# Nearest-neighbour upsampling: rows owned in two blocks, loads of 8, 252 and 252 rows, stores of at most 63 rows

## The chip, the cores and the metric

The kernel runs on one core of a Trainium2 chip. The metric is the device time of one execution in microseconds. Before the change three runs gave 197.04, 197.16 and 197.44 us, so the median is 197.16 us.

## The reference

Each element of `x` (16 × 64 × 64 × 64, float32) is written to a 2 × 2 square of the result, which is 16 × 64 × 128 × 128:

```python
for i in range(new_h):
    for j in range(new_w):
        src_i = i // scale_factor
        src_j = j // scale_factor
        result[:, :, i, j] = x[:, :, src_i, src_j].copy()
```

The input has 16.78 MB and the result 67.11 MB. Nothing is calculated: the work is moving bytes.

## The kernel before

The three outer dimensions of `x` are taken together into 65,536 rows of 64 elements (256 bytes). Each of the 128 partitions owns 512 rows that follow one another in memory. One row of `x` gives two rows of the result with 128 elements each, 1,024 bytes in all, so what a partition writes is contiguous as well: 512 × 1,024 bytes.

*Loads.* SyncE (SP) issues three loads: 8, 248 and 256 rows a partition (the cuts 0, 8, 256, 512). `begin_before_barrier` moves these three issues ahead of the barrier at the program's start.

*Copies.* VectorE (DVE) expands rows with a `tensor_copy` whose source repeats each element twice and each row twice (steps of 0), and whose destination is one dense stretch. A copy of k rows writes k × 256 elements a partition. The sizes stand in `rows`: 62, 32, 48, 64, 50, 64, 64, 64, 64. The first entry is copied in two halves, of 31 and 31 rows (`parts`). So there are ten copies. In this text copy 0 means the pair of 31 rows, and copy 1 to copy 8 are the others in order; store 0 to store 8 are the stores of what they wrote.

*Stores.* SP issues a store when the last copy into it is done, nine in all. Loads and stores share one queue and run in the order of their issue.

*Memory.* One SBUF tile `mem` holds a working area of 79 expanded rows and behind it all 512 source rows. Copies with an even number write at its start; copies with an odd number write a stretch that ends where the source rows that are not yet used begin. Two neighbours never overlap, but copy n overlaps what store n-2 reads, so copy n waits until store n-2 has landed. DVE runs the copies in order, so copy n also waits for copy n-1. Store n waits for copy n. In this way a copy has about the time of one store, that of number n-1, to be done before the queue runs empty.

`close_early` shortens the program's end and isn't touched.

Of the kernel before, what the change touches and what calls it, by code (L numbers as in the profile page):

```python
# [1 line left out]

# [4 lines left out]

EARLY = 3  # L10


def begin_before_barrier(nc):

    blocks = nc.main_func.blocks
    main, body = blocks[0], blocks[1]
    sp = mybir.EngineType.SP
    loads = [i for i in body.instructions if i.engine == sp][:EARLY]  # L20
    for load in loads:
        assert isinstance(load, mybir.InstDMACopy), type(load)
        assert not (load.sync_info and load.sync_info.on_wait)
    names = [i.name for i in loads]
    body.instructions = [i for i in body.instructions if i.name not in names]
    kept = list(main.instructions)
    at = next(
        n
        for n, i in enumerate(kept)
        if i.engine == sp and isinstance(i, mybir.InstDrain)  # L30
    )
    kept[at:at] = loads
    main.instructions = kept


def close_early(nc):

    blocks = nc.main_func.blocks  # L40
    sp, pool = mybir.EngineType.SP, mybir.EngineType.Pool
    stores = [
        i
        for i in blocks[1].instructions
        if i.engine == sp and isinstance(i, mybir.InstDMACopy)
    ]
    last = stores[-1].sync_info.on_update[0].id

    end = list(blocks[-1].instructions)
    wait = end[0]  # L50
    assert wait.engine == sp and isinstance(wait, mybir.InstDrain)
    waits = list(wait.sync_info.on_wait)
    assert len({w.id for w in waits}) == len(waits) > 2
    assert all(w.wait_mode == "sem-ge-imm" for w in waits)

    mine = [i for i in end if i.engine == pool]
    kinds = [type(i).__name__ for i in mine]
    assert kinds == [
        "InstDrain",
        "InstEventSemaphore",  # L60
        "InstEventSemaphore",
        "InstDrain",
        "InstISA",
        "InstDrain",
        "InstEventSemaphore",
        "InstEventSemaphore",
    ], kinds
    d0, gather0, release0, d1, clear, d2, gather1, release1 = mine


    lo, hi = clear.ant_dict["range_first"], clear.ant_dict["range_last"]
    assert lo <= last <= hi and all(lo <= w.id <= hi for w in waits)
    clears = []
    for a, b in ((lo, last), (last + 1, hi + 1)):
        if a < b:
            clears.append(nc.gpsimd.sem_clear(range(a, b)).ins)

    landed = mybir.InstDrain(
        name=wait.name,
        engine=pool,  # L80
        debug=wait.debug,
        sync_info=mybir.SyncInfo(
            on_wait=[w for w in waits if w.id != last], on_update=[]
        ),
    )
    (w,) = [w for w in waits if w.id == last]
    final = mybir.InstEventSemaphore(
        name=clear.name,
        engine=sp,
        debug=wait.debug,  # L90
        sync_info=mybir.SyncInfo(
            on_wait=[w],
            on_update=[
                mybir.SyncUpdate(
                    sync_type=w.sync_type,
                    id=w.id,
                    ant_name=w.ant_name,
                    update_mode="sem-sub-imm",
                    update_value=w.wait_value,
                )  # L100
            ],
        ),
    )
    others = [i for i in end if i.engine != pool and i is not wait]
    blocks[-1].instructions = others + [
        d0, gather0, release0, gather1, release1, d1, landed, *clears, d2, final
    ]


@with_exitstack  # L110
def kernel(
    ctx: ExitStack,
    tc: tile.TileContext,
    x: bass.AP,
    scale_factor: int,
    out: bass.AP,
):
    nc = tc.nc
    nc.at_finalize(begin_before_barrier)
    nc.at_finalize(close_early)  # L120
    P = nc.NUM_PARTITIONS
    s = int(scale_factor)
    B, C, H, W = x.shape
    R = B * C * H // P
    fdt = x.dtype

    xp = x.rearrange("b c h w -> (b c h) w").rearrange("(p r) w -> p r w", p=P)
    op = out.rearrange("b c (h hd) w -> (b c h) (hd w)", hd=s).rearrange(  # L130
        "(p r) w -> p r w", p=P
    )

    rows = [62, 32, 48, 64, 50, 64, 64, 64, 64]
    GROW = s * s
    FREE = 79
    WF = FREE * GROW * W  # L140
    assert sum(rows) == R
    mem_pool = ctx.enter_context(tc.tile_pool(name="mem", bufs=1))
    mem = mem_pool.tile([P, WF + R * W], fdt, name="mem")
    xt = mem[:, WF:].rearrange("p (r w) -> p r w", r=R)

    HEAD = 8
    cuts = [0, HEAD, R // 2, R]
    for lo, hi in zip(cuts, cuts[1:]):  # L150
        nc.sync.dma_start(out=xt[:, lo:hi], in_=xp[:, lo:hi])  # L151

    def expanded(r0, r1):
        return (
            xt[:, r0:r1].unsqueeze(2).unsqueeze(4).to_broadcast([P, r1 - r0, s, W, s])
        )

    r0 = 0
    before = (0, 0)
    for n, k in enumerate(rows):  # L160
        size = k * GROW * W
        at = 0 if n % 2 == 0 else WF + r0 * W - size
        assert at >= before[1] or at + size <= before[0]
        before = (at, at + size)
        u = mem[:, at : at + size].rearrange(
            "p (k a w b) -> p k a w b", k=k, a=s, w=W
        )
        parts = [0, 31, k] if n == 0 else [0, k]
        for a, b in zip(parts, parts[1:]):
            nc.vector.tensor_copy(out=u[:, a:b], in_=expanded(r0 + a, r0 + b))  # L170
        nc.sync.dma_start(out=op[:, r0 : r0 + k, :], in_=u)
        r0 += k


# [1 line left out]
_INS = ['x', 'scale_factor']  # L176
_OUTS = [((16, 64, 128, 128), 'float32')]

_NUMBERS = {'scale_factor': 2}


# [26 lines left out]
```

## Time and profile before

| what | value |
|---|---|
| time, median of three runs | 197.16 us |
| span of the profiled execution, first to last instruction | 195.8 us |
| what lies around the span (197.16 − 195.8) | 1.36 us |
| DVE busy | 78.0 us (40%), 10 copies |
| DMA, share of the 16 engines' time | 99.2% |
| DMA, bytes and mean rate | 83.89 MB, 428 GB/s |

For the profiled execution the page states its span alone; its own time, with what lies around the span, is not given, so the median of the three runs stands for it and the difference is taken as 1.36 us.

The page's numbers come from one execution. Its line on the DMA shows 40 equal slices of the span, and each digit is the busy share in tenths. The timeline lists instructions in order of time and merges neighbours of one kind ("x3"); in square brackets stands how long the engine had been idle before, and what released it. An SP row covers the issuing instructions, not the transfers.

### The profile page before, as it was taken

To read this page: it belongs to the slowest core of one execution; us is meant where nothing else is said; L and a number is where in the kernel's file an instruction comes from. 1 tells how busy PE (TensorE), PEld (TensorE's weight loads), DVE (VectorE), ACT (ScalarE), POOL (GpSimd) and SP (SyncE) were. 2 spreads that over 40 slices of the span, in tenths; PEclk is the share of its full clock that TensorE was granted. 3 is DMA by queue.
4 is the path that set the end of the run, shared out by engine and by line. 5 is a ranking of instruction groups with operands and counts; after the bars stand their busy time and mean duration, and the time that the engine had idled before them with its cause. 6 is when DMAs were issued, how large, how long until landed. Compare 5 with 4: busy or idle time off the path is not lost.

```text
span 195.8 us, 76 instructions
## 1 busy us (share of the span) xinstructions
DVE 78.0 (40%) x10; POOL 0.2 (0%) x4
## 2 busy tenths in 40 slices
DVE  0000599980007579085008907900890088000000
POOL 0000000000000000000000000000000000000000
DMA  9999999999999999899987989999999999999994
GB/s 456 415 428 415 428 428 428 428 415 415 415 415 428 428 482 482 375 469 495 469 384 345 502 348 455 442 469 482 469 442 428 428 428 442 428 428 428 428 428 214
DMA packets 1728, 83.89 MB, mean 428 GB/s; under 512 B 192, under 2 KB 192, under 8 KB 320
## 3 DMA queue, kind: packets, MB, share of 16 engines
q1 hardware_dynamic: 1728, 83.89, 99.2%
HBM read 16.78 MB, written 67.11 MB: 428 GB/s over the span
## 4 chain that ended last, share of the span: by engine, by line
DMA 60%; DVE 24%; SPq 0%; issue 0%; DVEq 0%
DMA out_dram<-mem 49%; DVE mem L170 24%; DMA mem<-in_x_dram 11%; SPq L151 0%; DVEq L170 0%
## 5 line engine op out<-in xcount | busy, mean ns | idle before, releaser
L170 DVE COPY mem<-mem 128x16384 f32<-128x16384 f32 (+4 forms) x10 | 78.0, 7812 | 87.8 <-DMA out_dram<-mem 65.8
L189 POOL MEMSET const-uint8-127<- 128x1 uint8 x1 | 0.1, 102 | 0.0
L189 POOL MEMSET const-bfloat16-1.0<- 128x1 bf16 x1 | 0.1, 101 | 0.0
L189 POOL MEMSET const-float32-0.0<- 128x1 f32 x1 | 0.1, 98 | 0.2 <-issue 0.2
L189 POOL MEMSET const-float32-1.0<- 128x1 f32 x1 | 0.1, 98 | 0.0
## 6 DMA issues: line engine op xcount, KB each, us to landing
mem<-in_x_dram SPq DMA_DIRECT2D x1, 7936.0 KB, 21.5
out_dram<-mem SPq DMA_DIRECT2D x1, 7936.0 KB, 21.2
out_dram<-mem SPq DMA_DIRECT2D x1, 6400.0 KB, 27.6
out_dram<-mem SPq DMA_DIRECT2D x1, 6144.0 KB, 17.5
out_dram<-mem SPq DMA_DIRECT2D x1, 4096.0 KB, 26.4
mem<-in_x_dram SPq DMA_DIRECT2D x1, 256.0 KB, 2.7
out_dram<-mem SPq DMA_DIRECT2D x5, 29.8
mem<-in_x_dram SPq DMA_DIRECT2D x1, 40.4
```

The costliest lines, as they stand in the source:

```text
L170: nc.vector.tensor_copy(out=u[:, a:b], in_=expanded(r0 + a, r0 + b))
L189: nc = _bacc.Bacc("TRN2", target_bir_lowering=False, num_devices=1)
```

## The change

The rows of `x` are cut into two parts. Of the first 128 × 260 rows each partition owns 260 that follow one another; of the other 128 × 252 rows each owns 252. So a partition's two stretches lie far apart in memory, and the distance between neighbouring partitions' stretches is 260 or 252 rows in place of 512. The loads become 8, 252 and 252 rows, and the sizes in `rows` become 62, 32, 52, 63, 51, 63, 63, 63, 63. The first five add up to 260, so no store crosses from one block into the other, and the number of loads (three), copies (ten) and stores (nine) is what it was. `within` cuts a stretch of rows at the blocks' border and returns the view of each piece.

```diff
-    xp = x.rearrange("b c h w -> (b c h) w").rearrange("(p r) w -> p r w", p=P)
-    op = out.rearrange("b c (h hd) w -> (b c h) (hd w)", hd=s).rearrange(
-        "(p r) w -> p r w", p=P
-    )
...
+    xr = x.rearrange("b c h w -> (b c h) w")
+    outr = out.rearrange("b c (h hd) w -> (b c h) (hd w)", hd=s)
+    BLOCKS = [260, 252]
+    assert sum(BLOCKS) == R
+    xb, ob, r0 = [], [], 0
+    for k in BLOCKS:
+        xb.append(xr[P * r0 : P * (r0 + k)].rearrange("(p r) w -> p r w", p=P))
+        ob.append(outr[P * r0 : P * (r0 + k)].rearrange("(p r) w -> p r w", p=P))
+        r0 += k
+
+    def within(views, lo, hi):
+        found, r0 = [], 0
+        for k, v in zip(BLOCKS, views):
+            a, b = max(lo, r0), min(hi, r0 + k)
+            if a < b:
+                found.append((a, b, v[:, a - r0 : b - r0]))
+            r0 += k
+        return found
+
+    rows = [62, 32, 52, 63, 51, 63, 63, 63, 63]
-    rows = [62, 32, 48, 64, 50, 64, 64, 64, 64]
...
-    HEAD = 8
-    cuts = [0, HEAD, R // 2, R]
-    for lo, hi in zip(cuts, cuts[1:]):
-        nc.sync.dma_start(out=xt[:, lo:hi], in_=xp[:, lo:hi])
+    LOADS = [0, 8, 260, R]
+    for lo, hi in zip(LOADS, LOADS[1:]):
+        for a, b, part in within(xb, lo, hi):
+            nc.sync.dma_start(out=xt[:, a:b], in_=part)
...
-        nc.sync.dma_start(out=op[:, r0 : r0 + k, :], in_=u)
+        for a, b, part in reversed(within(ob, r0, r0 + k)):
+            nc.sync.dma_start(out=part, in_=u[:, a - r0 : b - r0])
```

## The prediction

> **What bounds the kernel now.** I read the page's header first, then the slices and the DMA queue.
>
> ```profile
> span 195.8 us, 76 instructions
> DVE 78.0 (40%) x10; POOL 0.2 (0%) x4
> DVE  0000599980007579085008907900890088000000
> DMA  9999999999999999899987989999999999999994
> q1 hardware_dynamic: 1728, 83.89, 99.2%
> ```
>
> The 16 DMA engines are busy for 99.2% of the span, in every slice. DVE is busy for 40%. So the time is that of moving 83.89 MB, and a copy costs nothing as long as its store is issued before the queue runs empty. The question is therefore how much room each copy has. The timeline shows it.
>
> ```profile
> 0.00 1.32 SPq L151 DMA_DIRECT2D mem<-in_x_dram  x3
> 21.99 21.21 DVE L170 COPY mem<-mem 128x7936 f32<-128x7936 f32 x3 [21.99 <-DMA mem<-in_x_dram]
> 38.77 127.47 SPq L171 DMA_DIRECT2D out_dram<-mem  x9
> 59.98 6.56 DVE L170 COPY mem<-mem 128x12288 f32<-128x12288 f32 x1 [16.78 <-DMA out_dram<-mem]
> 69.70 8.70 DVE L170 COPY mem<-mem 128x16384 f32<-128x16384 f32 x1 [3.17 <-DMA out_dram<-mem]
> 84.12 6.83 DVE L170 COPY mem<-mem 128x12800 f32<-128x12800 f32 x1 [5.72 <-DMA out_dram<-mem]
> 103.54 8.69 DVE L170 COPY mem<-mem 128x16384 f32<-128x16384 f32 x1 [12.60 <-DMA out_dram<-mem]
> 118.55 8.69 DVE L170 COPY mem<-mem 128x16384 f32<-128x16384 f32 x1 [6.31 <-DMA out_dram<-mem]
> 137.94 8.70 DVE L170 COPY mem<-mem 128x16384 f32<-128x16384 f32 x1 [10.69 <-DMA out_dram<-mem]
> 157.19 8.69 DVE L170 COPY mem<-mem 128x16384 f32<-128x16384 f32 x1 [10.55 <-DMA out_dram<-mem]
> ```
>
> Each of the last seven rows begins when a store lands: copy 2 at the landing of store 0 (59.98), copy 3 at that of store 1 (69.70), and so on. From 59.98 to the end at 195.8 the queue moves the eight stores 1 to 8, 32+48+64+50+4×64 = 450 rows, so a stored row costs (195.8 − 59.98) / 450 = 0.3018 us. A row is 128 × 1,024 bytes, so that is 434 GB/s. A store of 64 rows takes 19.3 us and the copy beside it 8.7. The room is large.
>
> **The price of a copy.** This decides the case. The groups by shape:
>
> ```profile
> L170 DVE COPY mem<-mem 128x16384 f32<-128x16384 f32 x5 | 43.5, 8694 | 43.3 <-DMA out_dram<-mem 43.3
> L170 DVE COPY mem<-mem 128x7936 f32<-128x7936 f32 x2 | 16.7, 8414 | 22.0 <-DMA mem<-in_x_dram 22.0
> L170 DVE COPY mem<-mem 128x12800 f32<-128x12800 f32 x1 | 6.8, 6827 | 5.7 <-DMA out_dram<-mem 5.7
> L170 DVE COPY mem<-mem 128x12288 f32<-128x12288 f32 x1 | 6.6, 6561 | 16.8 <-DMA out_dram<-mem 16.8
> L170 DVE COPY mem<-mem 128x8192 f32<-128x8192 f32 x1 | 4.4, 4427 | 0.0
> ```
>
> Compare the second row with the last: 31 rows (7,936 elements) take 8,414 ns, 32 rows (8,192 elements) take 4,427 ns. Less work, almost twice the time. The rows with 64, 50, 48 and 32 rows lie on one line: slope (8694 − 4427) / (16384 − 8192) = 0.5209 ns an element, and 4427 − 8192 × 0.5209 = 160 ns fixed. With the same 160 ns the 31-row copies cost (8414 − 160) / 7936 = 1.040 ns an element, twice as much. The four fast sizes are even and the slow one is odd; all have the same line, types and source pattern, and the DMA is busy beside all of them. So I read it as: an odd number of rows halves DVE's rate. The change makes five copies of 63 rows and one of 51, both odd. By the odd rate 63 rows (16,128 elements) take 160 + 16128 × 1.040 = 16.94 us, where the even rate would give 8.56; 51 rows (13,056) take 13.74 instead of 6.96; 52 rows, even, take 7.09. The trace has only one odd size, so the lower bound of the price is the even rate, which gives the first rival.
>
> The Trainium skill says in "VectorE: DVE Perf Modes", section "What auto-detection actually checks", that a one-source copy in SBUF gets its two-elements-a-cycle mode if the outermost dimensions of source and destination are both even, or equal. Here the source's outermost count is the number of rows and the destination is one dense run, so by that rule 63 and 51 rows fall out of the mode as 31 do, and 62 rows in one copy would not. The rule reaches the sizes 63 and 51 that the trace doesn't show, and speaks against the change; by it the sum below stays as it is, and were the 31-row price a matter of size alone, the sum would be nothing.
>
> **What the change does not move.** Bytes, and the numbers of loads, copies and stores, stay the same. With the queue full, rows cost the same in any cut, so the new sizes by themselves cost nothing on the DMA. Load 2 has four rows more, at a quarter of a stored row's bytes each: 4 × 0.3018 / 4 = 0.30 us later, so copy 0 ends and store 0 is issued 0.30 us later, at 39.07. Load 3 covers that:
>
> ```profile
> L151 SPq DMA_DIRECT2D mem<-in_x_dram x3: 380/420/432, 0.0 to 0.9; - x3
> mem<-in_x_dram SPq DMA_DIRECT2D x1, 256.0 KB, 2.7
> mem<-in_x_dram SPq DMA_DIRECT2D x1, 40.4
> ```
>
> It is issued at 0.9 and lands 40.4 later, at 41.3, before and after alike, since the three loads together have the same bytes. The landings of stores 0 and 1, near 59.98 and 69.70, stay where they are. Were that cover gone, the price would be the 0.30 us. Copy 2 grows from 48 to 52 rows and ends at 59.98 + 7.09 = 67.07, while store 1 lands at about 69.63 (59.97 + 32 × 0.3018): covered too.
>
> **The price of an empty queue.** The trace of before never shows the queue run dry behind a store; the nearest case is the start. The first load is issued at 0.0 and lands at 2.7; its 256 KB are 0.60 us at 434 GB/s, which leaves 2.15 us on top (with 2.75 for the rounded 2.7). That is the upper bound, since it fetches from HBM with nothing in flight. The lower bound is the first packet alone, without a landing:
>
> ```profile
> DMA  0000000000000000000000000000000009929069
> ```
>
> These are 40 slices of the first 1.2 us: packets begin in slice 34, at 1.0 us. So a store into an empty queue pays L = 1.0 to 2.15 us, from its issue, beyond its rows. I take 1.6, the middle: it has a landing to wait for, which the lower bound leaves out, but reads SBUF and not HBM.
>
> **The sum, store by store.** A copy starts 0.08 us after the landing it waits for (the page's rows lie between 0.03 and 0.10: load 2's landing to 21.99 in the chain below, and 59.95 to 59.98), and its store is issued 0.03 after its end.
>
> ```profile
> 0.43 21.46 DMA mem<-in_x_dram
> 21.89 0.03 issue
> 21.99 16.76 DVE mem L170 x2
> 38.77 21.19 DMA out_dram<-mem
> 59.98 6.57 DVE mem L170
> 66.56 17.53 DMA out_dram<-mem
> ```
>
> - Copy 3 (63 rows) starts at 69.70 with store 1's landing and ends at 86.64; store 3 is issued at 86.67. Store 2 (52 rows) has landed at 69.63 + 52 × 0.3018 = 85.32. The queue is empty: store 3 counts from 86.67 + 1.6 = 88.27, which is 2.95 us late. It lands at 88.27 + 63 × 0.3018 = 107.29.
> - Copy 4 (51 rows) waits for copy 3 and ends at 100.39, while store 3 still runs: covered by 5.3 us. Store 4 lands at 107.29 + 15.39 = 122.68.
> - Copy 5 (63 rows) waits for store 3's landing, runs 107.37 to 124.30, issue 124.33. Store 4 has landed at 122.68. Empty again: 124.33 + 1.6 − 122.68 = 3.25 us late. Store 5 lands at 144.95.
> - Copy 6 waits for copy 5 (store 4 has landed) and ends at 141.25: covered by 2.1 us. Store 6 lands at 163.96.
> - Copies 7 and 8 wait for stores 5 and 6. Each turn takes 0.08 + 16.94 + 0.03 + 1.6 = 18.65 us against a store of 19.01: covered, by only 0.37 us.
>
> Two stalls, 2.95 + 3.25 = 6.2 us. They do not hide each other, for the queue has no spare time anywhere. The span becomes 195.8 + 6.2 = 202.0, and with the 1.36 us around it (median 197.16 less span 195.8) the time is 203.4 us. With L = 1.0 the sum is 1.35 + 1.65 + 2 × 1.0 = 5.0, time 202.2. With L = 2.15 it is 7.3, and copy 7 loses its cover too, by 0.18 us (copy 8 then has the late store 7 beside it): 7.5, time 204.7.
>
> **The rivals.**
>
> *The copies keep the even rate* (the not-slower case). The 31-row price would then come from something else about those two copies: they are the first, and they run while load 3 writes SBUF. Then 63 rows take 8.56 us, copy 3 ends at 78.3 against a landing at 85.3, every store is covered, and the time is 197.2. It decides from a copy time below 13.7 us (0.84 ns an element): copy 5 then fits, with 0.08 + 0.03 + 1.6, into store 4's 15.39. Against it: copy 1, with 32 rows, runs from about 38.8 while load 3 is still in flight until 41.3, and is fast. Chance 0.05.
>
> *The loop of waits never catches up.* If L is above 1.96 the turn of copy 7 runs dry as well. L = 2.4 gives 1.35 + 1.65 + 2 × 2.4 = 7.8, 0.43 for store 7 and 0.21 for store 0, which then comes after load 3 (39.07 + 2.4 against 41.26): 8.4 us in all, 205.6. For it: the 0.37 us of cover is thin. Against it: L's upper bound comes from a load. Chance above 204.7: 0.06.
>
> *The new distances between partitions speed up the transfers.* A partition's stretch lies 512 rows behind its neighbour's before, a power of two, and 260 or 252 after. If that had held transfers back, stores would shorten. The windows:
>
> ```profile
> 2.00:21.00 19.00, 0.00 (x0) 0.00 (x0) 1.00 1.02 436
> 103.00:157.00 54.00, 26.08 (x3) 0.00 (x0) 1.00 1.01 437
> ```
>
> The last column is GB/s. Loads (neighbours 128 KiB apart) move 436 and stores (512 KiB apart) 437, at a DMA share of 1: no sign that the wider distance costs anything. The best window against the mean of 434 leaves 0.7% for a gain, 0.2997 in place of 0.3018 us a row. As a mechanism: each store lands earlier, and so does the copy that waits for it start earlier, while the copies themselves stay as long, so the two stalls remain; the same working gives +5.4 us, 202.6. Only with the even copy rate as well would it be a gain, 512 × 0.0021 = 1.1 us, 196.1. A larger gain has no row that speaks for it. Chance that the transfers get faster at all: 0.03, with even copies 0.01 of it.
>
> The Trainium skill would make more of it: "DMA: Bandwidth & Descriptors", section "Latency and other measured facts", has copies between HBM tensors at a pitch of 512 KiB at 207 GB/s per direction, where 214 was the full rate. From its figures I estimate 3.3% a stored row, which gives 199.5 us with slow odd copies and 192.0 with fast ones; the two windows don't agree that this kernel pays it.
>
> **How the numbers follow.** The likeliest case (odd copies at half rate, two stalls) has 0.86; its time is 203.4 and its range 202.2 to 204.7 by the bounds of L. The three rivals take 0.05, 0.06 and 0.03. So the range holds 0.86 and need not reach to the first rival. About 0.2%, 0.4 us, is what a measurement of this kernel tells from no change. Slower: 0.86 + 0.06 + 0.02 = 0.94; same: 0.04; faster: 0.02 (0.01 for 196.1, and 0.01 of the first rival, for a shorter start).
>
> **What would show it.** Right: groups of 128x16128 with a mean near 16,940 ns and of 128x13056 near 13,740; DVE busy near 126.8 us (5 × 16.94 + 13.74 + 7.09 + 4.43 + 2 × 8.41, less their overlap); two slices or three near 85 to 88 and 122 to 126 us in which the DMA is not full; after that, idle DVE only in short gaps; copies 4 and 6 released by the copy before them and not by a store. Wrong: 16,128 elements in about 8,560 ns, or the odd copies slow and the DMA still full at 86 us, which would mean that L or the landings were misread; or a stored row whose cost differs from 0.3018 us between 145 and 200 us.

## The result and the profile after

The changed kernel takes 203.51 us (median of 5 runs, 203.07 to 203.62) against 197.04 us for the kernel before in the same job: 1.0318 of the time, 95% interval 1.0306 to 1.0330, so 6.5 us slower. The profiled execution took 203.54 us, and its span is 202.2 us, so 1.3 us lie around the span, about as was taken for the kernel before.

The page of the changed kernel, header, slices and queue:

```profile
span 202.2 us, 76 instructions
DVE 126.6 (63%) x10; POOL 0.2 (0%) x4
DVE  0000599960009499999907999999299959980000
DMA  9999999999989998699999794999999999999994
q1 hardware_dynamic: 1728, 83.89, 96.3%
```

The packets and bytes are those of before, but the engines are now busy for 96.3% of a longer span. The two deepest dips in the DMA's slices besides the end are a 6 (slice 17) and a 4 (slice 25). Both lie where DVE's slices show a 9. Windows over them (the last two columns are the DMA share and GB/s; packets count where they begin):

```profile
84.00:90.00 6.00, 6.00 (x2) 0.00 (x0) 1.00 0.40 172
121.00:128.00 7.00, 7.00 (x2) 0.00 (x0) 1.00 0.69 295
145.00:200.00 55.00, 33.91 (x2) 0.00 (x0) 1.00 1.00 432
```

In both windows DVE is busy without a break while the queue lacks work for a part of the time. From 145 us on the rate is full again. The groups by shape and the timeline say what DVE was doing:

```profile
L179 DVE COPY mem<-mem 128x16128 f32<-128x16128 f32 x5 | 84.7, 16951 | 15.4 <-DMA out_dram<-mem 15.4
L179 DVE COPY mem<-mem 128x13056 f32<-128x13056 f32 x1 | 13.7, 13744 | 0.0
L179 DVE COPY mem<-mem 128x13312 f32<-128x13312 f32 x1 | 7.1, 7093 | 16.5 <-DMA out_dram<-mem 16.5
```

```profile
60.22 7.09 DVE L179 COPY mem<-mem 128x13312 f32<-128x13312 f32 x1 [16.52 <-DMA out_dram<-mem]
70.02 30.61 DVE L179 COPY mem<-mem 128x16128 f32<-128x16128 f32 x2 [2.70 <-DMA out_dram<-mem]
107.58 33.81 DVE L179 COPY mem<-mem 128x16128 f32<-128x16128 f32 x2 [6.95 <-DMA out_dram<-mem]
145.12 16.95 DVE L179 COPY mem<-mem 128x16128 f32<-128x16128 f32 x1 [3.72 <-DMA out_dram<-mem]
164.10 16.95 DVE L179 COPY mem<-mem 128x16128 f32<-128x16128 f32 x1 [2.03 <-DMA out_dram<-mem]
```

51 rows (13,056 elements) take 13.7 us, and 52 rows (13,312) 7.1. The rows with "x2" are copies 3 and 4, and 5 and 6: the second of each pair begins at the end of the first, so it waited for DVE and not for a store. The two stalls can be measured from the chain of waits and the issues (KB, then us from issue to landing):

```profile
70.02 16.96 DVE mem L179
86.98 0.02 issue
87.00 20.46 DMA out_dram<-mem
...
107.58 33.82 DVE mem L179 x2
141.41 0.02 issue
141.42 22.65 DMA out_dram<-mem
```

```profile
out_dram<-mem SPq DMA_DIRECT2D x1, 6656.0 KB, 18.3
out_dram<-mem SPq DMA_DIRECT2D x1, 6528.0 KB, 22.2
```

Store 3 is issued at 87.00 and lands at 107.46. Its 63 rows are 19.01 us at 0.3018 a row, so the restart of the empty queue, from the issue, cost 20.46 − 19.01 = 1.45 us. Store 2 (6,656 KB) was issued at 60.22 + 7.09 + 0.02 = 67.33 and landed at 85.63, so store 3 came 107.46 − 19.01 − 85.63 = 2.82 us late. Store 4 (6,528 KB) was issued at 70.02 + 30.61 + 0.02 = 100.65 and landed at 122.85; store 5 landed at 145.03, if copy 7 (145.12) began 0.09 after it as copy 3 did after store 1 (69.93 and 70.02). So the second stall is 145.03 − 19.01 − 122.85 = 3.17 us. Together they are 5.99 of the span's 6.4 us, to about 0.1 us, since the times to landing are given in tenths.

### The profile page after: what moved, and what is told of

Read it like the earlier page. It is cut to its first block, busy times and chain, and to the rows that moved or that the text cites. A ratio compares the mean times of both kernels' runs of the same rounds, so it can differ in the third digit from the quotient of the medians.

```text
span 202.2 us, 76 instructions
## 1 busy us (share of the span) xinstructions
DVE 126.6 (63%) x10; POOL 0.2 (0%) x4
## 3 DMA queue, kind: packets, MB, share of 16 engines
q1 hardware_dynamic: 1728, 83.89, 96.3%
## 4 chain that ended last, share of the span: by engine, by line
DMA 45%; DVE 44%; SPq 0%; issue 0%; DVEq 0%
DVE mem L179 44%; DMA out_dram<-mem 34%; DMA mem<-in_x_dram 11%; SPq L160 0%; DVEq L179 0%
## 5 line engine op out<-in xcount | busy, mean ns | idle before, releaser
L179 DVE COPY mem<-mem 128x16128 f32<-128x16128 f32 (+4 forms) x10 | 126.6, 12685 | 54.5 <-DMA out_dram<-mem 31.9
```

## The experiments

### The other walk, for copies 1 to 8

The layout in blocks, the loads, the stores and all numbers of rows stay. The old walk goes row by row and writes both copies of a row before the next, so the number of rows is the outermost count. The other walk goes through all the rows once for the first copy and once more for the second, so the outermost count is 2.

```diff
+    def copied_first(r0, r1):
+        return (
+            xt[:, r0:r1].unsqueeze(1).unsqueeze(4).to_broadcast([P, s, r1 - r0, W, s])
+        )
...
+            if n > 0:
+                nc.vector.tensor_copy(
+                    out=u[:, a:b].rearrange("p k a w b -> p a k w b"),
+                    in_=copied_first(r0 + a, r0 + b),
+                )
+            else:
+                nc.vector.tensor_copy(out=u[:, a:b], in_=expanded(r0 + a, r0 + b))
```

> Blocks, loads, stores and all row numbers as in the changed kernel; copies 1 to 8 walk the two copies of a row in the outermost dimension (2) and the rows inside it, so that no outermost count is odd. Copy 0 stays as it is. Theory (an odd outermost count halves DVE's rate, and that alone makes the stalls): 63 rows in 0.16 + 16128 x 0.521 ns = 8.6 us instead of 16.95, no stall, span near 196.0, time near 197.3 us. Rival (63 rows are slow for their number or their place in memory, whatever the walk): 16.9 us a copy, time near 203.5. Rival (the new layout in blocks costs or gains time on the DMA): copies fast but the time off 197.0 by 0.4 us or more.

Measured: 197.35 us against 197.31 for the kernel before, ratio 0.999 (0.9969 to 1.0012). The groups of this run:

```profile
L185 DVE COPY mem<-mem 128x16128 f32<-128x16128 f32 x5 | 42.8, 8560 | 42.7 <-DMA out_dram<-mem 42.7
L190 DVE COPY mem<-mem 128x7936 f32<-128x7936 f32 x2 | 16.7, 8415 | 22.2 <-DMA mem<-in_x_dram 22.2
L185 DVE COPY mem<-mem 128x13056 f32<-128x13056 f32 x1 | 7.0, 6960 | 7.1 <-DMA out_dram<-mem 7.1
```

The same 16,128 elements, read and written at the same places, take 8,560 ns in place of 16,951. Only the order of the dimensions differs. The pair of 31 rows, which kept the old walk, is as slow as ever. So the price hangs on the walk with an odd outermost count and not on 63 rows as such, and with it the whole loss is gone. The blocks bring no gain and no cost that this interval can tell.

### The sizes alone, in the old layout

```diff
-    rows = [62, 32, 48, 64, 50, 64, 64, 64, 64]
+    rows = [62, 32, 52, 63, 51, 63, 63, 63, 63]
...
-    cuts = [0, HEAD, R // 2, R]
+    cuts = [0, HEAD, 260, R]
```

> The kernel before, 512 rows a partition in one stretch, with the changed kernel's row numbers (62, 32, 52, 63, 51, 63, 63, 63, 63) and its loads of 8, 252 and 252 rows. Theory: the odd numbers alone bring the loss; 63 rows in 16.95 us, two stalls of about 2.8 and 3.1 us, time near 203.3 us. Rival (the layout in blocks carries part of the loss, or hides a gain): the time differs from 203.5 us by 0.4 us or more, and the cost of a stored row differs from the changed kernel's.

Measured: 203.13 us, ratio 1.0298 (1.0273 to 1.0322), which overlaps the changed kernel's interval. Its span of 201.8 us is 0.4 shorter than the changed kernel's, and 0.35 of that stands before copy 2 (59.87 against 60.22). Its copies are the changed kernel's:

```profile
L170 DVE COPY mem<-mem 128x16128 f32<-128x16128 f32 x5 | 84.7, 16951 | 15.4 <-DMA out_dram<-mem 15.4
```

The numbers of rows bring the loss without the blocks, and the run before had the blocks without the loss.

### Only two of the six slow copies mended

The other walk for copies 3 and 5 alone:

```diff
-            if n > 0:
+            if n in (3, 5):
```

(The line with "-" is that of the first experiment, here and in the next one.)

> The changed kernel, with the other walk for copies 3 and 5 only; copies 4, 6, 7 and 8 stay odd and slow. Theory (a slow copy costs only where the store beside it is shorter than copy plus restart, which is behind the stores of 52 and 51 rows): both stalls gone, time near 197.3 us although DVE is busy for 110 us. Rival (all slow copies cost something, for instance because a chain of waits builds up): between 199 and 202 us.

Measured: 197.25 us, ratio 0.9993 (0.9980 to 1.0006). Its page, and then its groups:

```profile
DVE 110.0 (56%) x10; POOL 0.2 (0%) x4
```

```profile
L190 DVE COPY mem<-mem 128x16128 f32<-128x16128 f32 x3 | 50.9, 16953 | 10.9 <-DMA out_dram<-mem 10.9
L185 DVE COPY mem<-mem 128x16128 f32<-128x16128 f32 x2 | 17.1, 8559 | 8.0 <-DMA out_dram<-mem 8.0
```

DVE works 32 us longer than before the change (110.0 against 78.0) and the time is the same. Three copies of 63 rows and the one of 51 are still slow and cost nothing: the stores beside them are long enough.

### Only one of the two stalls mended

```diff
-            if n > 0:
+            if n == 3:
```

> The changed kernel, with the other walk for copy 3 only. Theory: store 3 is in time, so only the stall behind the store of 51 rows is left, 0.11 + 16.95 + 1.45 (restart, as measured in the changed kernel) - 15.4 = 3.1 us; time near 200.3 us. Rival (one stall feeds the next, so that the first mended mends both, or the second grows by what the first leaves): 197.3, or over 202.

Measured: 200.49 us against 197.12, ratio 1.0171 (1.0158 to 1.0184), so 3.4 us. In its timeline copy 3 is fast, and copies 5 and 6 still follow one another without a pause:

```profile
69.66 8.56 DVE L185 COPY mem<-mem 128x16128 f32<-128x16128 f32 x1 [2.64 <-DMA out_dram<-mem]
104.38 33.81 DVE L190 COPY mem<-mem 128x16128 f32<-128x16128 f32 x2 [5.36 <-DMA out_dram<-mem]
```

About half of the loss is left. The second stall alone costs about what it costs behind the first, so the two add. The first one alone, with copy 5 mended, was not run.

### The same sizes in another order

```diff
-    rows = [62, 32, 52, 63, 51, 63, 63, 63, 63]
+    rows = [62, 32, 52, 51, 63, 63, 63, 63, 63]
```

> The changed kernel with the fourth and fifth row numbers exchanged (62, 32, 52, 51, 63, then four of 63): the same odd sizes, the same slow copies, the same bytes. Theory: the copy of 51 rows (13.7 us) now runs beside the store of 52 rows (15.7) and fits, at 70.0 + 13.75 + 1.45 = 85.2 against a landing at 85.4; the copy of 63 rows behind it runs beside the store of 51 and makes the one stall of 3.1 us; time near 200.3 us. Rival (the loss goes with DVE's busy time or the number of odd copies): 203.5 us as before.

Measured: 200.39 us, ratio 1.0169 (1.0156 to 1.0182), with the same slow copies (84.8 us of DVE time for those of 63 rows). The timeline of this run:

```profile
69.68 13.75 DVE L179 COPY mem<-mem 128x13056 f32<-128x13056 f32 x1 [2.64 <-DMA out_dram<-mem]
85.31 33.94 DVE L179 COPY mem<-mem 128x16128 f32<-128x16128 f32 x2 [1.88 <-DMA out_dram<-mem]
```

The copy of 51 rows ends at 83.43, and the next copy is released by store 2, 1.88 us later. So store 3, issued as soon as the copy of 51 rows had ended, was in time. Only the pairing of a copy with the store beside it changed, and half of the loss went.

### Even numbers in the two blocks

```diff
-    rows = [62, 32, 52, 63, 51, 63, 63, 63, 63]
+    rows = [62, 32, 52, 62, 52, 62, 64, 62, 64]
```

> The changed kernel's two blocks and its loads, with even numbers of rows (62, 32, 52, 62, 52 and 62, 64, 62, 64) and the old walk. Theory: copies near 8.4 to 8.7 us, no stall, time within 0.4 us of the kernel before, so neither better nor worse. Rival (blocks gain on the DMA): under 196.8 us.

Measured: 197.36 us against 197.12, ratio 1.0008 (0.9999 to 1.0017): no difference from the kernel before that can be told. Its group of 62 rows, in the old walk:

```profile
L179 DVE COPY mem<-mem 128x15872 f32<-128x15872 f32 x3 | 25.3, 8427 | 24.5 <-DMA out_dram<-mem 24.5
```

62 rows take half the time of 63. None of the mended versions is faster than the kernel before.

### The first copy in one piece

In the kernel before, copy 0 is two odd halves. In one piece it is even.

```diff
-        parts = [0, 31, k] if n == 0 else [0, k]
+        parts = [0, k]
```

> The kernel before, with copy 0 as one copy of 62 rows instead of two of 31. Theory: 15872 elements, even, take 0.16 + 15872 x 0.521 ns = 8.43 us instead of 16.76 for the pair; store 0 is issued 8.3 us earlier, behind load 3 that still runs, so the time stays at 197.1 us within 0.3. Rival (the two first copies are slow because they are the first, or run beside load 3): the one copy takes about 16.7 us.

Measured: 198.30 us, ratio 1.0056 (1.0035 to 1.0077). The price of the copy came out as expected, the time did not. The timeline of this run, its group of 62 rows, and its row for load 3 (us from issue to landing):

```profile
21.79 12.89 DVE L170 COPY mem<-mem 128x15872 f32<-128x15872 f32 x2 [21.79 <-DMA mem<-in_x_dram]
30.24 137.15 SPq L171 DMA_DIRECT2D out_dram<-mem  x9
```

```profile
L170 DVE COPY mem<-mem 128x15872 f32<-128x15872 f32 x1 | 8.4, 8427 | 21.8 <-DMA mem<-in_x_dram 21.8
```

```profile
mem<-in_x_dram SPq DMA_DIRECT2D x1, 41.4
```

62 rows take 8,427 ns at the very place, beside load 3, where 31 rows took 8,414. That ends the rival that the first two copies are slow for where they stand. But load 3 lands 41.4 us after its issue, where it was 40.4, and the kernel loses 1.0 us although its copies got faster. The next three runs look into that.

### The first copy in one piece, with its store held back

The copy of 62 rows is made twice over, the second time in whole (store 0 is then issued at 38.6 us), for its first 32 rows (34.9 us) or for 50 rows (37.7 us). Copy 1 and store 1, which follow, move with store 0. Shown is the first of the three; in the others the second pair is (0, 32) or (0, 50).

```diff
-        parts = [0, 31, k] if n == 0 else [0, k]
-        for a, b in zip(parts, parts[1:]):
+        parts = [(0, k), (0, k)] if n == 0 else [(0, k)]
+        for a, b in parts:
```

> The kernel before, with copy 0 as one copy of 62 rows that is made twice, so that it is even and fast but store 0 is issued at about 38.8 us as before. In the run with one copy of 62 rows store 0 was issued at 30.2, and the last packets of load 3 took 3.5 to 4.0 us instead of 2.4. Theory (a store that is queued early behind a load makes the change from loading to storing dearer): the loss of 1.0 us is gone, time near 197.2 us. Rival (the copy of 62 rows in one instruction, or its pattern, is what costs): 198.3 us again.

> The kernel before, copy 0 as one copy of 62 rows whose first 32 rows are then written a second time, so that store 0 is issued at about 21.8 + 8.4 + 4.4 = 34.7 us; load 3's last packets begin at 37.7 to 38.3. Theory (a switch: the change from loading to storing is dear as soon as the store is queued well before load 3's last packets): the full 1.0 us, time near 198.2 us, last packets of load 3 near 3.5 to 4 us. Rival (the loss grows with the time that the store was queued): about half, near 197.7 us.

> As the run before, with 50 rows written a second time: store 0 is issued at about 37.1 us, 0.6 us before load 3's last packets begin and before a store that is issued into an empty queue would count (1.45 us). Theory of the switch: no loss, near 197.1 us, if the store's first reads come after load 3's last packets began; the full 1.0 us if being issued is enough. Rival (the loss grows with the time queued): 0.2 us, near 197.3.

Measured: 197.02 us, ratio 1.0001 (0.9988 to 1.0015), with the store at 38.6; 198.58 us, ratio 1.0081 (1.0051 to 1.0111), at 34.9; 198.44 us, ratio 1.0057 (1.0031 to 1.0084), at 37.7. For each, in this order, store 0's issue in the chain of waits:

```profile
38.62 21.14 DMA out_dram<-mem
```

```profile
34.90 26.47 DMA out_dram<-mem
```

```profile
22.40 8.44 DVE mem L170
...
37.72 24.32 DMA out_dram<-mem
```

And in the same order load 3's time to landing:

```profile
mem<-in_x_dram SPq DMA_DIRECT2D x1, 40.1
```

```profile
mem<-in_x_dram SPq DMA_DIRECT2D x1, 41.7
```

```profile
mem<-in_x_dram SPq DMA_DIRECT2D x1, 42.4
```

It is not the one instruction of 62 rows that costs, nor its shape: with the store held to 38.6 the loss is gone. It does not grow with the time that the store was queued either: the store at 37.7 loses as much as those at 30.2 and 34.9, where 0.2 us was expected if the loss grew with that time. In the run at 37.7 load 2 itself was 0.4 us later (copy 0 at 22.40 against 21.99 in the kernel before), so of the 2.0 us by which its 42.4 exceeds the 40.4, some 2.0 − 0.4 = 1.6 us are load 3's. That profile is of an execution of 199.25 us, 0.8 above the run's median, so 1.6 us is more than most of its executions lost. The limit lies between 37.7 and 38.6 us, by one profile on each side.

## Why the prediction was right

*The odd copies* were the step that carried it, and they hold: 16.95 and 13.74 us were measured for 16.94 and 13.74 forecast, and DVE's busy time is 126.6 us for 126.8. The rule had one odd size behind it; the other walk and the even numbers show now that the count's being odd is the cause.

*Where they cost.* The two places came out as forecast, behind the stores of 52 and 51 rows. Mending those two copies (197.25 us) removes everything, mending one (200.49) or changing the order (200.39) removes half.

*The restart* was mis-sized a little: L was taken as 1.6 us, between 1.0 and 2.15, and measured 1.45. That the middle of so wide a range came within 0.15 us is in part luck, for no row of the old profile showed a store into an empty queue. So the stalls are 2.82 and 3.17 us where 2.95 and 3.25 stood, 0.2 less together.

*What made up for it.* Store 0 lands 0.24 us later than in the profile of before (copy 2 at 60.22 against 59.98), where no shift was forecast. This looks like the start's scatter and not like the change, for the first experiment has the same blocks and loads, and in its timeline copy 2 begins at 59.91:

```profile
59.91 7.09 DVE L185 COPY mem<-mem 128x13312 f32<-128x13312 f32 x1 [16.51 <-DMA out_dram<-mem]
```

And a stored row costs a trace more: from store 6's landing at 164.07 to the end, 126 rows take 202.2 − 164.07 = 38.1 us, 0.3026 each, which is 0.15 us over the last three stores. 5.99 + 0.24 + 0.15 is the span's 6.4 us. So 203.4 against 203.51 owes its last tenths to errors that cancel.

*The rivals.* The even rate for odd copies fell with the groups. The loop that never catches up fell too: copies 7 and 8 were in time, as the full rate from 145 us on shows. A faster transfer from the new distances between partitions fell with the three runs that have the blocks and fast copies where it matters: 0.999, 0.9993 and 1.0008 of the time before. The estimate of 3.3% from the Trainium skill's "DMA: Bandwidth & Descriptors", section "Latency and other measured facts", gave 192.0 us for fast copies and doesn't show here: these three runs took 197.35, 197.25 and 197.36 us. The Trainium skill's condition in "VectorE: DVE Perf Modes", section "What auto-detection actually checks", agrees with every kernel of this case: with the rows outermost the odd counts 31, 51 and 63 run at half rate and the even ones at the full rate, and with the outermost count 2 every number of rows that was tried (32, 51, 52 and 63) is fast.

## What to carry to other kernels

Before changing a tile's size look for an instruction whose time doesn't fit its size: one odd row in the groups of the old profile (31 rows slower than 32) gave the price of all six slow copies here. If an odd size is wanted, walk the tile so that the outermost dimension is even. In this kernel a slower engine beside a full queue cost only where the transfer that covers it was shorter than the instruction plus the restart, so look at each pair of neighbours and not at the busy share.

## What had not been expected of the hardware

A store that is issued early can cost time. With store 0 queued at 37.7 us or before, ahead of the end of load 3, load 3 landed 1.0 to 1.6 us later in the profiles and the kernel was slower by 0.6 to 0.8%; with the store at 38.6 to 39.0 us nothing was lost. The windows around this place, first of the run with the store at 30.2, then of the one with it at 38.6 (last column GB/s):

```profile
38.00:46.00 8.00, 0.00 (x0) 0.00 (x0) 1.00 0.81 319
```

```profile
38.00:46.00 8.00, 5.02 (x2) 0.00 (x0) 1.00 0.99 430
```

Packets count where they begin, so windows as short as these exaggerate: over 40 to 60 us the rates are 406 and 433 GB/s. The packets of loads and stores share the queue either way, and what makes the change from one to the other dear was not found, nor was store 0 moved without copy 1 and store 1. Later stores are queued long before their turn without such a loss (in the kernel before copy 7 ends at 146.6 us, and store 6 lands, for copy 8, at 157.2), but they follow stores. So the two slow halves of copy 0 in the kernel before do a service: they hold store 0 back until load 3 is nearly done.
